# A hybrid decoder layer: other first loads, five-panel weight rings, and low-rank stages at other places of TensorE's order

## The chip, the cores and the metric

The kernel runs on one core of a Trainium2 chip. The metric is the time of one execution on the device in microseconds (us), and the smaller is the better. A core has a matrix engine (TensorE, called PE in the profile), a vector engine (VectorE, DVE), an engine for functions and copies (ScalarE, ACT), one for general work (GpSimd, POOL), and a synchronising engine (SyncE, SP) that here only issues transfers. They run side by side, each through its own list of instructions in order, and wait for each other by semaphores. Transfers from the device's memory (DMA) run beside all of them.

## The reference

One layer for 256 tokens of width 2048. A root-mean-square norm, one product into all branch inputs, four causal window averages (pooling), a recurrent mixer of 16 heads of 64 (RWKV-7), an output product, a squared-ReLU network of width 8192, and a gated embedding:

```
h = rms_norm(x, attn_norm);  z = h @ w_in
d = causal_multiscale_pool(z_pool);  pool_out = (d @ pool_w) * pool_scale
zs = token_shift(z[...], mu_shift)                # r, k, v and the low-rank w, a, g
y = rwkv7_time_mix(zs...)                         # state S <- S*w + (S a) b^T + v k^T,  y = S r
x = x + concatenate([pool_out, y]) @ w_out
x = x + square(relu(rms_norm(x, mlp_norm) @ w_ffn_up)) @ w_ffn_down
gate = sigmoid(rms_norm(x, ple_norm) @ w_ple_gate)
x = x + gate * (p @ w_ple_proj);  return rms_norm(x, final_norm)
```

All is computed in 32-bit floats.

## The kernel before

**Products.** A large product takes each 32-bit operand apart into a high part, rounded to TensorE's fast 32-bit type (fp32r), and the low rest, and adds three products: high by high, low by high, high by low. Weights come in panels of 512 KB, 128 partitions by 1024. `load_raw` issues the transfer on SP's queue, `split_w` (lines L157 to L166) makes the high part on ACT in two halves (`wh`, L165) and the low part on DVE (`wl`, L166). The buffers of raw, high and low panels are rings (`ring`): three of each, and one more of each once the mixer's memory is free, each fourth panel going there. A panel can be loaded when the last reader of the buffer's former panel is done.

**Stages.** The head (0 to 26.5 us of the trace) loads x transposed (`xT`, four panels of four k-tiles of 128 rows) and a narrow weight `wag` of 288 columns for the low-rank inputs w, a and g, multiplies them in plain 32-bit floats (`wag_prod`, two matmuls for each k-tile, which the trace shows as four records), squares x on DVE, sums the squares over partitions by four small matmuls (`sbank`), takes the root (`rs_n`), spreads the factors over partitions by two matmuls (`s_ps`, `s_bc`) and scales and splits x into `hTh` and `hTl`.

Then come the products of `w_in` in the order zk, zr for heads' group 0, zk, zr for group 1, zv0, zv1, zp0, zp1 (26.5 to 275). They are generators in a queue. Between their pieces the stages of the mixer are put: `fill(us)` issues products for about so many microseconds by the author's estimate, and `finish(gen)` all that is left of one. The stages of a group of eight heads are `rwkv_lora` (low-rank decay and a: two banks lw and la, sigmoids, a scan, two exponentials), `rwkv_k` (kkn, rnb), `rwkv_r`, `rwkv_scores` (sc), `rwkv_sources` (bkt), `bonus_sums` (bsum), `rwkv_values` (bon, vt), `rwkv_core` (us, dy), `group_norm`, and `group_out` (yt: a transposition). A triangular inverse runs on DVE beside them. A product's two banks are evacuated by `shift_evac` (L322 on ACT, L323 on DVE). Up to here TensorE's order is that of the code; DVE's and ACT's are set by a scheduler by priorities (`tc.high_priority`).

After the output product (287 to 384) the network goes in two halves. Each half has a product up (L1104, L1108; 384 to 564 and 731 to 911) and two sweeps down (`sweep`, 564 to 731 and 911 to 1068), over 16 pairs of panels. A plain pair (even ones, and 15) is split as above. A seven pair (odd ones from 1 to 13) uses seven products where eight would stand: `weights_seven` forms four combinations of its panels ra and rb on DVE (t1, which is two of them, L1226; t2, L1231; t3, L1232), and the parts `w7h`, `th` (ACT) and `w7l` (L1229, L1235), `tl` (L1236) (DVE). Behind the last seven pair, `u` combines the banks, and `scaled_residual` adds them to x, the wide one for 1024 columns at once. The gate's product and the end follow (1068 to 1191). Eight of the gate's panels are split early and kept (`keep`), in memory whose tags `keep_at` names.

Of the kernel before, what the change touches and what calls it, by code (L numbers as in the profile page):

```python
# [9 lines left out]
F32 = mybir.dt.float32  # L10
# [30 lines left out]
def trunk(  # L41
# [39 lines left out]
    def rw_bank(name):  # L81
        return psr.tile([128, 512], F32, tag="rw", name=name)
# [19 lines left out]
    nc.vector.memset(ones, 1.0)  # L102
# [227 lines left out]
    order.enter_context(tc.manual_schedule(engines={mybir.EngineType.PE}))  # L330
    wag_banks = [rw_bank(f"wag_b{i}") for i in range(2)]
# [20 lines left out]
    def load_wag(tag, k0, n, eng=nc.sync):  # L352
        wr = rp.tile([128, n, 288], F32, tag=tag, name=f"wag{k0}")
        eng.dma_start(wr, w_wag[:, k0 : k0 + n, :])
        return [wr[:, i, :] for i in range(n)]
# [8 lines left out]
    def load_wags(eng, *parts):  # L364
        for tg, k0, n in parts:
            wr.update(zip(range(k0, k0 + n), load_wag(tg, k0, n, eng)))
# [17 lines left out]
    for k in range(12):  # L384
        wag_prod(k)
# [6 lines left out]
    for k in range(12, 14):  # L392
        wag_prod(k)
# [14 lines left out]
    for k in range(14, NK):  # L408
        wag_prod(k)
# [602 lines left out]
    fill(14.0)  # L1012
    st0 = rwkv_lora(0)
    finish(p_zk0)
    wband = make_bands()
    rwkv_k(0, st0, zk0[0])
# [18 lines left out]
    finish(p_zv0)  # L1035
    fill(4.0)
    rwkv_values(0, st0, zv0[0])
    bonus_sums(1, st1)
# [15 lines left out]
    fill(4.0)  # L1054
# [98 lines left out]
    keep_at = ["ys"] * 3 + ["a5", "th", "tl", "t", "U"]  # L1153

    def keep():
# [3 lines left out]
        if where == "ys":  # L1159
            wh, wl = (fp.tile([128, 1024], F32R, tag=where, bufs=7, name=f"gk{kp}{c}") for c in "hl")  # L1160
# [55 lines left out]
    def weights_seven(ra, rb, name):  # L1216
# [7 lines left out]
        with tc.high_priority(20000):  # L1224
# [4 lines left out]
            nc.vector.tensor_tensor(la, ra, ha.bitcast(F32), op=ALU.subtract)  # L1229
# [269 lines left out]
```

## Time and profile before

| | us |
|---|---|
| three timed runs | 1195.39, 1196.88, 1192.28 |
| median | 1195.39 |
| the profiled execution's own time | 1192.48 |
| its span, first to last instruction | 1190.8 |
| busy in it: PE, DVE, ACT | 1164.7, 855.4, 678.7 |

The profile shows one execution. A line of the timeline gives start, time taken, engine, source line, operation, output and inputs with their shapes, how many instructions are grouped (x16), and in square brackets the idle time ahead of them and what ended it. A 32-bit matmul of the head is two records. A matmul's own time reaches into the next one's, so that the distance from start to start is its cost. PEclk is the share of TensorE's full clock that was granted.

### The profile page before, as it was taken

What the parts mean: (1) busy time and instruction counts of PE and PEld (TensorE: products, weight loads), DVE (VectorE), ACT (ScalarE), POOL (GpSimd) and SP (SyncE); (2) the same over time, 40 slices, a digit from 0 to 9 for tenths busy, and PEclk for the clock granted to TensorE, in tenths of its full rate; (3) what the DMA queues carried; (4) which work ended last, traced back from release to release, by engine and by line L of the source; (5) the groups of instructions that cost most, each with busy time, mean ns of one, the idle gap of its engine ahead of it and who ended that gap; (6) DMA issues with size and microseconds to landing.
All of it is one profiled execution on the core that took longest, in us unless ns stands there. A gap on an engine that the chain in (4) does not pass through costs nothing.

```text
span 1190.8 us, 18955 instructions
## 1 busy us (share of the span) xinstructions
PE 1164.7 (98%) x7366; PEld 996.4 (84%) x7366; DVE 855.4 (72%) x1073; ACT 678.7 (57%) x1210; POOL 20.1 (2%) x77
## 2 busy tenths in 40 slices
PE   7999999999999999999999999999999999999997
PEld 5899999787888888888878888888888788887886
DVE  6885799356655666667788887666668789888753
ACT  5956765667555554555554554554546554568643
POOL 4100000000000000000000000000000000000000
PEclk9999999999999999999999999999999999999999
DMA  7353434454566556565455656555555565666831
GB/s 267 124 187 124 155 125 142 143 175 138 191 184 191 178 180 191 182 190 182 172 212 185 217 204 210 193 181 190 185 187 163 208 208 186 218 246 201 274 125 71
DMA packets 60618, 216.92 MB, mean 182 GB/s; under 512 B 6768, under 2 KB 7536, under 8 KB 60144
## 3 DMA queue, kind: packets, MB, share of 16 engines
q1 hardware_dynamic: 60240, 215.20, 54.8%
q8 instruction: 58, 0.95, 0.3%
q10 hardware_dynamic: 288, 0.51, 0.1%
q14 instruction: 32, 0.26, 0.1%
HBM read 213.59 MB, written 2.10 MB: 181 GB/s over the span
## 4 chain that ended last, share of the span: by engine, by line
PE 73%; DVE 5%; DMA 2%; ACT 1%; issue 1%; DVEq 0%; ACTq 0%
PE u_w L1104 20%; PE d_p L1173 13%; PE u_w L1108 10%; PE d_w L1173 5%; PE d_d L1173 3%; PE o_b L188 2%; PE o_b L187 2%; PE o_b L189 2%; PE gt_b L187 2%; PE gt_b L189 2%; PE gt_b L188 2%; DVE wl_d L166 2%; DMA raw_d<-in_w_ffn_down_dram 2%; PE zp_b L187 1%; PE zp_b L189 1%
## 5 line engine op out<-in xcount | busy, mean ns | idle before, releaser
L1104 PE MATMUL u_w<-h,wh_u 128*128 128x512 f32 x1024 | 362.1, 399 | 0.0
L1108 PE MATMUL u_w<-h,wl_u 128*128 128x256 f32 x1024 | 287.7, 281 | 0.0
L165 ACT ACTIVATE wh_u<-raw_u 128x512 fp32r<-128x512 f32 x256 | 147.4, 624 | 175.6 <-issue 136.7
L166 DVE TENSOR_TENSOR wl_u<-raw_u,wh_u 128x1024 fp32r<-128x1024 f32 x128 | 156.6, 1224 | 120.9 <-ACT wh_u L165 120.9
L1104 PEld LDWEIGHTS u_w<-h,wh_u 128*128 128x128 f32 x1024 | 192.5, 188 | 47.8
L1108 PEld LDWEIGHTS u_w<-h,wl_u 128*128 128x128 f32 x1024 | 193.4, 189 | 0.0
L1173 PE MATMUL d_p<-wh_d,yd 128*128 128x512 f32 x432 | 115.6, 389 | 0.0
L1173 PEld LDWEIGHTS d_p<-wh_d,yd 128*128 128x128 f32 x432 | 81.0, 188 | 16.6
L165 ACT ACTIVATE wh_d<-raw_d 128x512 fp32r<-128x512 f32 x144 | 79.7, 619 | 23.4 <-PE d_d L1173 12.0
L166 DVE TENSOR_TENSOR wl_d<-raw_d,wh_d 128x1024 fp32r<-128x1024 f32 x72 | 85.1, 1219 | 2.3 <-ACT wh_d L165 2.2
L1236 DVE TENSOR_TENSOR tl_d<-t_d,th_d 128x2048 fp32r<-128x2048 f32 x28 | 64.2, 2292 | 29.3 <-ACT th_d L1234 29.3
L1173 PE MATMUL d_p<-wl_d,yd 128*128 128x512 f32 x216 | 68.5, 393 | 2.8 <-DVE wl_d L166 2.8
L1234 ACT ACTIVATE th_d<-t_d 128x1024 fp32r<-128x1024 f32 x28 | 29.7, 1060 | 69.1 <-DVE t_d L1232 69.1
L166 DVE TENSOR_TENSOR wl_o<-raw_o,wh_o 128x1024 fp32r<-128x1024 f32 x32 | 39.1, 1225 | 35.9 <-ACT wh_o L165 35.9
L165 ACT ACTIVATE wh_o<-raw_o 128x512 fp32r<-128x512 f32 x64 | 36.7, 624 | 32.4 <-PE o_b L188 18.4
L1173 PEld LDWEIGHTS d_p<-wl_d,yd 128*128 128x128 f32 x216 | 40.5, 188 | 14.2 <-DVE wl_d L166 6.1
L1226 DVE TENSOR_TENSOR t_d<-raw_d,raw_d 128x1024 f32<-128x1024 f32 x28 | 34.2, 1222 | 14.4 <-DMA raw_d<-in_w_ffn_down_dram 14.4
L1173 PE MATMUL d_w<-th_d,ys 128*128 128x512 f32 x168 | 42.6, 389 | 0.0
L1230 ACT ACTIVATE th_d<-t_d 128x1024 fp32r<-128x1024 f32 x28 | 29.7, 1060 | 17.9 <-DVE t_d L1226 14.7
L178 PE MATMUL zv_b<-hTh,wh_zv 128*128 128x256 f32 x128 | 37.8, 295 | 1.3 <-DVE zv_t L323 1.3
L178 PE MATMUL zr_b<-hTh,wh_zr 128*128 128x256 f32 x128 | 36.7, 287 | 2.0 <-DVE zk_t L323 2.0
L1173 PE MATMUL d_d<-wh_d,yd 128*128 128x512 f32 x144 | 38.5, 389 | 0.0
(445 smaller groups left out, 2529.5 us busy)
## 6 DMA issues: line engine op xcount, KB each, us to landing
raw_u<-in_w_ffn_up_dram SPq DMA_DIRECT2D x128, 512.0 KB, 3.5
raw_d<-in_w_ffn_down_dram SPq DMA_DIRECT2D x128, 512.0 KB, 4.4
raw_o<-in_w_out_dram SPq DMA_DIRECT2D x32, 512.0 KB, 3.5
raw_gt<-in_w_ple_gate_dram SPq DMA_DIRECT2D x24, 512.0 KB, 4.4
raw_zk<-in_w_in_dram SPq DMA_DIRECT2D x16, 512.0 KB, 4.1
raw_zr<-in_w_in_dram SPq DMA_DIRECT2D x16, 512.0 KB, 3.5
raw_zv<-in_w_in_dram SPq DMA_DIRECT2D x16, 512.0 KB, 3.5
raw_zp<-in_w_in_dram SPq DMA_DIRECT2D x16, 512.0 KB, 3.5
```

The source lines that it names most:

```text
L165: nc.scalar.activation(wh[:, a * 512 : (a + 1) * 512], raw[:, a * 512 : (a + 1) * 512], AF.Copy)
L166: nc.vector.tensor_tensor(wl, raw, wh.bitcast(F32), op=ALU.subtract)
L178: nc.tensor.matmul(o, w_h, ah, start=first and ct % 2 == 0, stop=False, skip_group_check=True)
L187: nc.tensor.matmul(o, a_h, wh[:, 0:n], start=first, stop=False)
L188: nc.tensor.matmul(o, a_l, wh[:, 0:n], start=False, stop=False)
L189: nc.tensor.matmul(o, a_h, wl[:, 0:n], start=False, stop=last)
L1104: nc.tensor.matmul(bank[:, ct, :].rearrange("p (s t) -> p s t", s=2), wh[:, c], hl, start=k == 0, stop=False, skip_group_check=True,)
L1108: nc.tensor.matmul(bank[:, ct, 0:T], wl[:, c], hl[:, 0, :], start=False, stop=k == 15, skip_group_check=True)
L1173: nc.tensor.matmul(o, l, r, start=first, stop=last, skip_group_check=True)
L1226: nc.vector.tensor_tensor(t[:, 0:2], ra.rearrange("p (c n) -> p c n", c=2), b12.unsqueeze(1).to_broadcast([128, 2, 512]), op=ALU.subtract)
L1230: nc.scalar.activation(th[:, 0:2], t[:, 0:2], AF.Copy)
L1236: nc.vector.tensor_tensor(tl, t, th.bitcast(F32), op=ALU.subtract)
```

## The change

It has three parts.

1. *Head.* `ones` is written earlier; nine matmuls of `ones` by `ones` into a bank of their own stand ahead of TensorE's other work. The first x^T panel comes in two halves, the first three k-tiles of wag as two (on ACT's queue) and one; the last two x^T panels are issued ahead of wag's k-tiles 9 to 11. The four matmuls of the norm's sum stand behind eleven k-tiles of wag, not twelve, the two of s_ps behind thirteen, not fourteen.
2. *Rings and the sweeps.* Raw, high and low panels have three buffers and two more (low: one more) after the mixer. `u` uses the memory of t, and `keep_at` another place in the list. In `weights_seven` the DVE part of ra's low half stands behind t2 and t3. The wide residual's priority is 25000, not 10000.
3. *Mixer's order.* `rwkv_lora(0)` stands behind the end of zk0, `rwkv_lora(1)` ahead of `rwkv_sources(0)`, `bonus_sums(1)` right behind the end of zv0; three fill times differ.

```diff
-    nc.vector.memset(ones, 1.0)
+    with tc.high_priority(40000):
+        nc.vector.memset(ones, 1.0)
...
+    RING = {"raw": (3, 2), "wh": (3, 2), "wl": (3, 1)}
     def ring(tag, dt, name):
-        if extra:
-            turns[tag] += 1
-            if turns[tag] % 4 == 0:
-                return extra[0].tile([128, 1024], dt, tag=f"{tag}x", name=name)
-        return wp.tile([128, 1024], dt, tag=tag, name=name)
+        n, m = RING[tag]
+        turns[tag] += 1
+        if extra and turns[tag] % (n + m) >= n:
+            return extra[0].tile([128, 1024], dt, tag=f"{tag}x", bufs=m, name=name)
+        return wp.tile([128, 1024], dt, tag=tag, bufs=n, name=name)
...
+    warm_bank = rw_bank("warm_b")
+    for i in range(9):
+        nc.tensor.matmul(warm_bank[:, 0:128], ones, ones, start=True, stop=True)
...
+    def load_wag(tag, k0, n, eng=nc.sync, first=0):
+        wr_ = rp.tile([128, n, 288], F32, tag=tag, name=f"wag{k0}")
+        if first:
+            nc.scalar.dma_start(wr_[:, 0:first], w_wag[:, k0 : k0 + first, :])
+        eng.dma_start(wr_[:, first:n], w_wag[:, k0 + first : k0 + n, :])
+        return [wr_[:, i, :] for i in range(n)]
...
-    load_wags(nc.scalar, ("tE", 0, 3))
-    load_xT(0, 0, 4)
-    load_wags(nc.sync, ("tF", 3, 3))
+    load_xT(0, 0, 2)
+    load_wags(("tE", 0, 3), first=2)
+    load_xT(0, 2, 2)
+    load_wags(("tF", 3, 3))
     load_xT(1, 0, 4)
-    load_wags(nc.sync, ("zk", 6, 3))
+    load_wags(("zk", 6, 3))
     load_xT(2, 0, 4)
-    load_wags(nc.sync, ("zr", 9, 3))
     load_xT(3, 0, 4)
-    load_wags(nc.sync, ("zv", 12, 2), ("BK", 14, 2))
+    load_wags(("zr", 9, 3), ("zv", 12, 2), ("BK", 14, 2))
...
-    for k in range(12):
+    for k in range(11):
         wag_prod(k)
...
-    for k in range(12, 14):
+    for k in range(11, 13):
...
-    for k in range(14, NK):
+    for k in range(13, NK):
...
-    fill(14.0)
-    st0 = rwkv_lora(0)
     finish(p_zk0)
     wband = make_bands()
+    fill(3.0)
+    st0 = rwkv_lora(0)
+    fill(3.0)
     rwkv_k(0, st0, zk0[0])
...
     rwkv_scores(0, st0)
+    st1 = rwkv_lora(1)
     rwkv_sources(0, st0)
     bonus_sums(0, st0)
-    st1 = rwkv_lora(1)
     finish(p_zk1)
     rwkv_k(1, st1, zk1[0])
-    fill(12.0)
+    fill(13.0)
     rwkv_scores_half(1, st1, 0)
...
     finish(p_zv0)
+    bonus_sums(1, st1)
     fill(4.0)
     rwkv_values(0, st0, zv0[0])
-    bonus_sums(1, st1)
...
-    fill(4.0)
+    fill(5.3)
     for gi in range(2):
         group_out(gi, 1, norms[1][gi], YTs[gi])
...
-    keep_at = ["ys"] * 3 + ["a5", "th", "tl", "t", "U"]
+    keep_at = ["ys"] * 3 + ["yd", "a5", "th", "tl", "t"]
...
-            nc.vector.tensor_tensor(la, ra, ha.bitcast(F32), op=ALU.subtract)
-            nc.scalar.activation(th[:, 0:2], t[:, 0:2], AF.Copy)
             nc.vector.tensor_tensor(t[:, 2], b22, t[:, 0], op=ALU.add)
             nc.vector.tensor_tensor(t[:, 3], b21, t[:, 2], op=ALU.subtract)
+            nc.scalar.activation(th[:, 0:2], t[:, 0:2], AF.Copy)
             nc.scalar.activation(hb[:, 0:512], b21, AF.Copy)
+            nc.vector.tensor_tensor(la, ra, ha.bitcast(F32), op=ALU.subtract)
+            nc.vector.tensor_tensor(lb[:, 0:512], b21, hb[:, 0:512].bitcast(F32), op=ALU.subtract)
             nc.scalar.activation(th[:, 2:4], t[:, 2:4], AF.Copy)
-            nc.vector.tensor_tensor(lb[:, 0:512], b21, hb[:, 0:512].bitcast(F32), op=ALU.subtract)
...
-                    u = fp.tile([128, 4, 512], F32, tag="U", name=f"u_{name}")
+                    u = fp.tile([128, 4, 512], F32, tag="t", name=f"u_{name}")
...
-        with tc.high_priority(10000 if wide > 512 else 30000):
+        with tc.high_priority(25000 if wide > 512 else 30000):
```

Line numbers of the changed kernel are higher by 2 to 9: the splits L165 and L166 are L167 and L168, t1, t2, t3 are L1235, L1238, L1239, the low halves L1242 and L1243.

The first place is ACT's list in the head, from the last scaling of x^T (tD) to the first high part of h; `wh_zk_0`, `_1` and `_2` are the first three panels of zk. Before:

```order
L341 ACTIVATE tD_t<-xq_204,par_sb 128x256 x4
L165 ACTIVATE wh_zk_0_343<-raw_zk_0_341 128x512 x2
L165 ACTIVATE wh_zk_1_374<-raw_zk_1_372 128x512 x2
L165 ACTIVATE wh_zk_2_426<-raw_zk_2_424 128x512
L398 ACTIVATE rs_n_288<-sbank,eps_n 128x2
L165 ACTIVATE wh_zk_2_426<-raw_zk_2_424 128x512
L407 ACTIVATE s_bc<-s_ps 128x256
L170 ACTIVATE hTh_152<-tA_t 128x256 x2
```

And in the changed kernel:

```order
L346 ACTIVATE tD_t<-xq_214,par_sb 128x256 x4
L405 ACTIVATE rs_n_298<-sbank,eps_n 128x2
L167 ACTIVATE wh_zk_0_355<-raw_zk_0_353 128x512 x2
L167 ACTIVATE wh_zk_1_386<-raw_zk_1_384 128x512
L414 ACTIVATE s_bc<-s_ps 128x256
L167 ACTIVATE wh_zk_1_386<-raw_zk_1_384 128x512
L172 ACTIVATE hTh_152<-tA_t 128x256
L167 ACTIVATE wh_zk_2_438<-raw_zk_2_436 128x512
L172 ACTIVATE hTh_152<-tA_t 128x256
L167 ACTIVATE wh_zk_2_438<-raw_zk_2_436 128x512
```

The norm's root (`rs_n`) has moved ahead of all of zk's high parts, which so start behind sbank, and the first two k-tiles of h are taken one by one between the parts of the third panel.

The second place is TensorE's list ahead of the second half of the groups' outputs (`yt`), from the last window average (`pd`) to the gates (`gt`); `zp_b` is the last product of the queue. Before:

```order
L951 MATMUL pd_3391<-wband,zt_2918 128x128
L890 MATMUL yt<-ident,ys_2746 128x128 x4
L890 MATMUL yt<-ident,ys_2747 128x128 x4
L187 MATMUL zp_b_2928<-wh_zp_7_3330,hTh_153 128x512
L188 MATMUL zp_b_2928<-wh_zp_7_3330,hTl_155 128x512
L189 MATMUL zp_b_2928<-wl_zp_7_3331,hTh_153 128x512
L187 MATMUL zp_b_2928<-wh_zp_7_3330,hTh_153 128x512
L188 MATMUL zp_b_2928<-wh_zp_7_3330,hTl_155 128x512
L189 MATMUL zp_b_2928<-wl_zp_7_3331,hTh_153 128x512
L890 MATMUL yt<-ident,ys_2746 128x128 x4
L890 MATMUL yt<-ident,ys_2747 128x128 x4
L909 MATMUL gt<-zf,gu_2715 128x256 x4
```

And in the changed kernel:

```order
L958 MATMUL pd_3411<-wband,zt_2911 128x128
L897 MATMUL yt<-ident,ys_2764 128x128 x4
L897 MATMUL yt<-ident,ys_2765 128x128 x4
L897 MATMUL yt<-ident,ys_2764 128x128 x4
L897 MATMUL yt<-ident,ys_2765 128x128 x4
L916 MATMUL gt<-zf,gu_2733 128x256 x4
```

The six products of zp between the two halves of yt are gone from here; they stand ahead of the places shown, and no product of the queue is left for `fill(5.3)`.

The third place is DVE's list in the first sweep down, around the plain pair 8 and the seven pair 9: `t_d_9` are t1, t2 and t3, `wl_d_0_8` and `wl_d_1_8` the low parts of pair 8, `w7l_d_9` and `tl_d_9` those of pair 9. Before:

```order
L1236 TENSOR_TENSOR tl_d_7_6248<-t_d_7_6246,th_d_7_6247 128x2048
L166 TENSOR_TENSOR wl_d_0_8_6289<-raw_d_0_8_6284,wh_d_0_8_6288 128x1024
L166 TENSOR_TENSOR wl_d_1_8_6294<-raw_d_1_8_6286,wh_d_1_8_6293 128x1024
L1226 TENSOR_TENSOR t_d_9_6326<-raw_d_0_9_6322,raw_d_1_9_6324 128x1024
L1229 TENSOR_TENSOR w7l_d_9_6331<-raw_d_0_9_6322,w7h_d_9_6329 128x1024
L1231 TENSOR_TENSOR t_d_9_6326<-raw_d_0_9_6322,t_d_9_6326 128x512
L1235 TENSOR_TENSOR w7l_d_9_6332<-raw_d_1_9_6324,w7h_d_9_6330 128x512
L1232 TENSOR_TENSOR t_d_9_6326<-raw_d_1_9_6324,t_d_9_6326 128x512
L1236 TENSOR_TENSOR tl_d_9_6328<-t_d_9_6326,th_d_9_6327 128x2048
```

And in the changed kernel:

```order
L1245 TENSOR_TENSOR tl_d_7_6260<-t_d_7_6258,th_d_7_6259 128x2048
L1235 TENSOR_TENSOR t_d_9_6338<-raw_d_0_9_6334,raw_d_1_9_6336 128x1024
L1238 TENSOR_TENSOR t_d_9_6338<-raw_d_0_9_6334,t_d_9_6338 128x512
L168 TENSOR_TENSOR wl_d_0_8_6301<-raw_d_0_8_6296,wh_d_0_8_6300 128x1024
L168 TENSOR_TENSOR wl_d_1_8_6306<-raw_d_1_8_6298,wh_d_1_8_6305 128x1024
L1239 TENSOR_TENSOR t_d_9_6338<-raw_d_1_9_6336,t_d_9_6338 128x512
L1242 TENSOR_TENSOR w7l_d_9_6343<-raw_d_0_9_6334,w7h_d_9_6341 128x1024
L1243 TENSOR_TENSOR w7l_d_9_6344<-raw_d_1_9_6336,w7h_d_9_6342 128x512
L1245 TENSOR_TENSOR tl_d_9_6340<-t_d_9_6338,th_d_9_6339 128x2048
```

t1 and t2 of pair 9 have moved ahead of pair 8's low parts, and the low part of pair 9's first panel behind t3. In the first sweep of each half this is so at the seven pairs 3, 5, 7, 9, 11 and 13 (t1 and t2 ahead of both low parts, or of the first), in the second at 11 and 13; before, t1 alone was ahead at 3, 5, 7 and 11, and in the second sweep at 11.

More of the change, by code (lines that the diff above doesn't have):

```diff
@@ L350, in squares @@
         return sq
[L352 to L355, printed above, removed]
+    def load_wag(tag, k0, n, eng=nc.sync, first=0):
[4 more added lines that the diff above has]
+        return [wr_[:, i, :] for i in range(n)]
     def wag_prod(k):
@@ L362, in wag_prod, with load_wags @@
             )
[L364 removed]
+    def load_wags(*parts, first=0):
         for tg, k0, n in parts:
[L366 removed]
+            wr.update(zip(range(k0, k0 + n), load_wag(tg, k0, n, nc.sync, first)))
     wr = {}
[L369 to L371 removed]
+    load_xT(0, 0, 2)
+    load_wags(("tE", 0, 3), first=2)
+    load_xT(0, 2, 2)
+    load_wags(("tF", 3, 3))
     load_xT(1, 0, 4)
[L373 removed]
+    load_wags(("zk", 6, 3))
     load_xT(2, 0, 4)
[L375 removed]
     load_xT(3, 0, 4)
[L377 removed]
+    load_wags(("zr", 9, 3), ("zv", 12, 2), ("BK", 14, 2))
     sums = []
@@ L1158, in keep @@
         raw = load_raw(w_gate[3, kp].rearrange("p a n -> p (a n)"), 1024, f"gk{kp}")
-        if where == "ys":
-            wh, wl = (fp.tile([128, 1024], F32R, tag=where, bufs=7, name=f"gk{kp}{c}") for c in "hl")
+        if where[0] == "y":
+            wh = fp.tile([128, 1024], F32R, tag="ys", bufs=7, name=f"gk{kp}h")
+            wl = fp.tile([128, 1024], F32R, tag=where, bufs=7 if where == "ys" else 1, name=f"gk{kp}l")
         else:
```

## The prediction

> **What bounds the kernel now.** I read the page first (share of each engine), then the waits of TensorE, then the stages by windows, then single places in the timeline. Columns of the waits: who waits at which line, for whom, us in total, times, longest.
>
> ```profile
> span 1190.8 us, 18955 instructions
> PE 1164.7 (98%) x7366; PEld 996.4 (84%) x7366; DVE 855.4 (72%) x1073; ACT 678.7 (57%) x1210; POOL 20.1 (2%) x77
> PE wag_b L359 <- DMA wag<-in_w_wag_dram: 7.8, 1, 7.8
> PE d_p L1173 <- DVE wl_d L166: 2.8, 6, 0.6
> PE zr_b L178 <- DVE zk_t L323: 2.0, 1, 2.0
> PE sc L642 <- DVE AR L584: 1.4, 1, 1.4
> PE zv_b L178 <- DVE zv_t L323: 1.3, 1, 1.3
> PE yt L890 <- DVE gv L883: 1.2, 1, 1.2
> ```
>
> TensorE (PE) is busy 98% of the span, so 1190.8 - 1164.7 = 26.1 us is all that its waits can give back, and 7.8 of them are the start. The change adds or removes no product of the body: its gain must come out of these 26 us, out of products that ran at half clock, or both.
>
> ```profile
> core 0: us, PE busy (x) PEld busy (x) DVE busy (x) ACT busy (x) POOL busy (x), PEclk, DMA share, GB/s
> 112.00:206.00 94.00, 91.28 (x963) 87.42 (x963) 81.52 (x144) 58.96 (x109) 1.12 (x2) 0.98 0.41 135
> 384.00:564.00 180.00, 180.00 (x1023) 156.25 (x1022) 120.06 (x162) 96.66 (x179) 0.00 (x0) 1.00 0.59 185
> 564.00:648.00 84.00, 82.94 (x364) 67.84 (x363) 69.44 (x66) 45.42 (x67) 0.00 (x0) 1.00 0.55 188
> ```
>
> In the FFN-up stage (384 to 564) PE has no gap at all: deeper rings and other orders can change nothing there. The waits lie in the head, in the mixer (27 to 287) and in the four FFN-down sweeps, the first from 564 to 648. I go through these.
>
> **The head, part 1 of the change.** Timeline of PE: start, time taken, what.
>
> ```profile
> 7.84 6.09 PE L359 MATMUL wag_b<-wag,tA_t 128*128 128x288 f32 x16 [7.84 <-DMA wag<-in_w_wag_dram]
> 13.77 4.04 PE L359 MATMUL wag_b<-wag,tB_t 128*128 128x288 f32 x16
> 17.65 4.04 PE L359 MATMUL wag_b<-wag,tC_t 128*128 128x288 f32 x16
> 21.53 0.95 PE L388 MATMUL sbank<-ones,sqx 128*128 128x1 f32 x8
> 24.36 0.61 PE L406 MATMUL s_ps<-dgs,ones 128*128 128x128 f32 x4
> 26.54 0.49 PE L178 MATMUL zk_b<-hTh,wh_zk 128*128 128x256 f32 x1
> ```
>
> The second row's sixteen records start 17.65 - 13.77 = 3.88 us before the third, 0.2425 each; the first row's take 13.77 - 7.84 = 5.93. So 2.05 us go to a half-speed clock at the start. From 7.84 on PE never waits until zk. In the changed kernel 64 records of 0.2425 (15.5), sbank's 0.8 and s_ps's 0.45 are the same work, 16.8 us; only the start and the cold clock move. The first pieces are two k-tiles of x^T (256 KB in place of 512) and two of wag (288 KB in place of 432), on two queues as before; I put the first product at 6.7, between 7.84, where a smaller load brings nothing, and 6.0, where the row of ACT below has its first scaled k-tile (start 5.60, a quarter of 1.70), with parameters and x^T there but for the weights; 6.7 because the weights, the last to land, are a third smaller. The nine products of ones are 18 records; at twice s_ps's 0.11 they run from the end of the memset, 1.2, to about 5.2. If they leave the clock at full speed, zk starts at 6.7 + 16.8 = 23.5. ACT and DVE must follow:
>
> ```profile
> 5.60 1.70 ACT L341 ACTIVATE tA_t<-xq,par_sb 128x256 f32<-128x256 f32 x4 [2.86 <-DMA par_sb<-in_par_dram]
> 16.70 0.42 DVE L383 TENSOR_TENSOR sqx<-sqx,sqx 128x256 f32<-128x256 f32 x1
> 25.01 0.38 ACT L407 ACTIVATE s_bc<-s_ps 128x256 f32<-128x256 f32 x1 [1.71 <-PE s_ps L406]
> ```
>
> The squares end at 17.1 and sbank now comes after eleven k-tiles, 6.7 + 44 x 0.2425 = 17.4: no wait. In the new order rs_n stands ahead of zk's weight splits on ACT, and one split of DVE (1.2 us) ahead of the low half of h: s_ps 20.7, s_bc 21.2, product 21.8, split 23.0, low half 23.7. So zk is fully fed at about 23.6: **-2.9 us**, bounds -0.9 (clock still cold) and -3.6 (first product at 6.0).
>
> [...]
>
> **The mixer, part 3.** Four waits are touched.
>
> ```profile
> 49.99 1.28 ACT L530 ACT_TABLE_LOAD   x1
> 51.36 1.06 ACT L530 ACTIVATE tA_t<-tB_t 128x1024 f32<-128x1024 f32 x1
> 118.11 1.28 ACT L530 ACT_TABLE_LOAD   x1
> 126.48 1.28 ACT L543 ACT_TABLE_LOAD   x1
> 54.32 0.28 PE L180 MATMUL zr_b<-hTh,wl_zr 128*128 128x256 f32 x1
> 56.59 0.39 PE L178 MATMUL zr_b<-hTh,wh_zr 128*128 128x256 f32 x1 [1.99 <-DVE zk_t L323]
> 137.52 0.28 PE L180 MATMUL zv_b<-hTh,wl_zv 128*128 128x256 f32 x1
> 139.19 2.00 PE L642 MATMUL sc<-AR,BK 64*128 64x64 f32 x32 [1.39 <-DVE AR L584]
> 142.88 0.41 PE L178 MATMUL zv_b<-hTh,wh_zv 128*128 128x256 f32 x1
> 274.67 0.40 PE L189 MATMUL zp_b<-wl_zp,hTh 128*128 128x512 f32 x1
> 276.28 0.63 PE L890 MATMUL yt<-ident,ys 128*128 128x128 f32 x4 [1.22 <-DVE gv L883]
> ```
>
> (1) zr's second bank (56.59) waits for the evacuation of zk's first, which sits on ACT behind lora's sigmoids, a table load and two exponentials. In the new order lora(0) stands 27 products behind zk's last, so the evacuations come first: **-2.1** (0 if lora's work runs into the next evacuation instead).
>
> (2) sc (139.19) waits for AR, at the end of a chain through k(1), while ACT loads its table four times, for lora(1) and k(1) in turn (first and last are the rows 118.11 and 126.48). lora(1) now stands ahead of sources(0), so its exponentials are over when k(1) begins, which takes two of the four loads (2 x 1.28) and lora's own work off that chain; fill(13) adds one us of cover. 1.4 of waiting against 2.6 + 1.0: the wait goes, with its tail **-1.5**. Behind it PE ran at half clock: products of 0.41 in place of 0.28 (row 142.88), and the window's clock of 0.98. (1 - 0.98) x 94 gives 1.9; sixteen products some 0.09 late give 1.5. I hold the idle time to be its cause: **-1.5**, bounds 0 and -1.9.
>
> [...]
>
> (3) The second bank of zv's second part waits 1.3 for DVE, which evacuates the first part behind the inverse's steps. bonus_sums(1), four products of up to 256 columns that stood behind it, now stands ahead of it, as cover: 0.5 by products of 0.12 us, and the rest if DVE's steps shift with it. I take **-0.7**, bounds 0 and -1.3.
>
> (4) yt waits for the group norm. Before, six zp products (1.4 us) stood between its two halves. The new order has none left there, as it used them up earlier; fill(5.3) finds an empty queue. The norm's chain is as long as before, so the wait grows by those six: **+1.4**. A pause of some 2.7 us can re-gate the clock as at 139: half a chance of 1.6, **+0.8**.
>
> (5) lora(0) inside zr leaves fewer products between rnb and scores(0): 99 where 159 stood. No row shows that wait; the nearest is the same wait of group 1, 1.4, below it nothing: **+0.4**.
>
> **FFN down, part 2.** DVE, the loop of one seven pair (odd) and a plain pair (even), 593 to 599, and ACT's next start; ahead of them the two loads' rows of the page, their last column the us from issue to landing:
>
> ```profile
> raw_u<-in_w_ffn_up_dram SPq DMA_DIRECT2D x128, 512.0 KB, 3.5
> raw_d<-in_w_ffn_down_dram SPq DMA_DIRECT2D x128, 512.0 KB, 4.4
> 587.37 0.69 DVE L1232 TENSOR_TENSOR t_d<-raw_d,t_d 128x512 f32<-128x512 f32 x1
> 593.19 1.23 DVE L1226 TENSOR_TENSOR t_d<-raw_d,raw_d 128x1024 f32<-128x1024 f32 x1 [1.72 <-DMA raw_d<-in_w_ffn_down_dram]
> 594.33 2.35 DVE L166 TENSOR_TENSOR wl_d<-raw_d,wh_d 128x1024 fp32r<-128x1024 f32 x2
> 598.94 0.68 DVE L1232 TENSOR_TENSOR t_d<-raw_d,t_d 128x512 f32<-128x512 f32 x1
> 604.92 0.63 ACT L1233 ACTIVATE w7h_d<-raw_d 128x512 fp32r<-128x512 f32 x1 [1.86 <-DMA raw_d<-in_w_ffn_down_dram]
> ```
>
> The stall reads so: DVE's t1 (L1226) waits for its panel, the plain pair's low halves (L166) stand behind it, and PE waits for those. A panel is issued when the last reader of its buffer is done: with four buffers t3 (L1232) of the seven pair before, 588.1, landed 593.2: 5.1 us; the next 599.6 to 604.9, 5.3. From t1 to t3's end are 6.4 us, so a pair of pairs with t1 first takes 11.4 or more, against PE's 45 products (24 in a plain pair, 21 in a seven pair) of 0.228 (82.94 us by 364, the windows' row) = 10.3; where L166 comes first it takes less, and on average DVE keeps up. Six stalls of 0.5 to 0.6 (the waits' row), with restarts some 4.6 us in all.
>
> The new order puts t1 and t2 ahead of both low halves at 16 of the 28 seven pairs, where t1 alone was ahead at ten. With five buffers the panel that t1 needs waits for the high pair's low half (L1229), which stands behind t1, t2, two L166 and t3: all that fills the 6.4 us now but one half panel (0.6), so 5.8 to 5.9. The two panels of a pair are no longer issued together. With the median landing, 4.4, the loop is 10.3, PE's own, with nothing to spare: I allow 0.16 at each of 16 places, 2.6; with 3.5, the landing in the stage without waits, it is 9.4 and no stall is left. From 4.6 to 2.6: **-2.0**, bounds -4.6 and, at 5.3 (0.9 over in 16 places, 14.4), +9.8.
>
> The scale's higher priority for wide residuals and u in t's place put DVE's work at a sweep's end a few us earlier or later beside products of the other banks; I see no wait there now and take 0, as for keep's new places, which PE reads 80 us later.
>
> **Sum.** -2.9 - 2.1 - 1.5 - 1.5 - 0.7 + 1.4 + 0.8 + 0.4 - 2.0 = -8.1. The profiled execution took 1192.48 (span 1190.8 and 1.7 around it), which gives 1184.4. It lies 2.9 below the median of the three timed runs, 1195.39; a median of new runs may sit anywhere in that spread, so I add half of it: **1185.8**.
>
> **Rivals.** (a) The clock stays or falls cold: the products of ones end about 1.5 us before the first wag product. Then the head gives 0.9: 1187.8. For it: the half clock behind 139.19 after as short a pause. Against: that pause had sparse products ahead.
> (b) The mixer makes new waits: scores(0) at the full 1.4 in place of 0.4, zv's kept (0.7), yt's clock lost in full (0.8), together 2.5 more: 1188.3. For it: lora's table load is only moved, beside another chain.
> (c) The rings do not do what they are for: DVE's order is static, t1 stays ahead, stalls remain 4.6: 1187.8.
> (d) **Slower than before**: DVE's t1 and t2 at the head of the line. A landing of 5.3, as twice above, makes the loop 11.2, 0.9 over PE's at 16 places: +9.8 where I have -2.0, so 1197.6, and more where it is longer still. It decides from a landing of about 5.1, where 0.7 at 16 places less the 4.6 are +6.6 and eat up the rest of the gain. For it: 5.1 and 5.3 are what this loop shows now. Against it: both were panels issued right behind their partners, which five buffers take apart.
>
> **How the numbers follow.** A measurement of this kernel can tell about 0.5%, 6 us, from no change; faster means below 1189.4, slower above 1201.4. Forecast 0.45, (a) 0.17, (b) 0.15, (c) 0.13, (d) 0.10. (b) lies close to the line, a third of it beyond; (d) lies inside it but for landings above 5.5. Faster 0.78, same 0.18, slower 0.04. The range takes the favourable bounds (head 0.7, FFN 2.6, yt's clock 0.8, zv 0.6 better and the fast half of the spread, 1.5: about 1179.6) and above it (a) to (c) two at a time, and a part of (d): 1192.5.
>
> **What would show it.** Right: zk's first product near 23.6; the second sixteen records no slower than the first; no wait at zr's second bank or at sc; one wait of 2.5 to 3 at yt; d_p's wait for wl_d below 2. Wrong: wag's first row at 5.9 again (a); a wait at the scores of group 0 (b); six or more waits of d_p (c), or some sixteen with t_d waiting for raw_d by over 1 us each (d).

## The result, and the profile after

| | before | changed |
|---|---|---|
| median of 12 runs each, us | 1195.13 | 1189.31 |
| lowest to highest | 1191.08 to 1196.88 | 1187.06 to 1192.90 |
| ratio, 95% interval | | 0.9961 [0.9948, 0.9974] |
| profiled execution's own time | 1192.48 | 1192.90 |

The change is faster by 0.39%, 4.7 us (the ratio is that of the means; the medians lie 5.8 apart), within the 6 us that the prediction called no change; the forecast had 8 to 10. The two profiled executions happen to take the same time, since that of before is one of its faster ones and that of the changed kernel its slowest. So the profiles show where time moved, and the timed runs how much it is.

The waits of TensorE in the changed kernel (who waits at which line, for whom, us in total, times, longest):

```profile
PE yt L897 <- DVE gv L890: 3.3, 1, 3.3
PE zk_b L180 <- DVE zr_t L325: 2.2, 1, 2.2
PE zr_b L180 <- DVE zk_t L325: 1.9, 1, 1.9
PE zp_b L189 <- DVE zv_t L325: 1.6, 1, 1.6
PE warm_b L335 <- DVE ones L103: 1.2, 1, 1.2
PE rnb L496 <- DVE rnq L560: 0.9, 2, 0.7
PE us L852 <- ACT UV L845: 0.9, 1, 0.9
PE vt L776 <- DVE ybuf L762: 0.9, 1, 0.9
PE zv_b L180 <- DVE zv_t L325: 0.4, 1, 0.4
PE wag_b L366 <- DMA wag<-in_w_wag_dram: 0.3, 1, 0.3
PE d_p L1182 <- DVE wl_d L168: 0.2, 1, 0.2
```

The start's 7.8 and the sweeps' 2.8 are gone, and sc's 1.4. zr's 2.0, which was to go, is still there. New are waits at zk's second bank, zp, rnb and us; vt's has grown from 0.2 to 0.9 and yt's from 1.2 to 3.3. All of them lie in the mixer. The stages of the same profile:

```profile
27.00:112.00 85.00, 80.74 (x718) 76.62 (x716) 61.31 (x93) 58.87 (x114) 3.78 (x12) 0.96 0.43 142
112.00:206.00 94.00, 90.54 (x917) 86.02 (x915) 81.50 (x142) 55.62 (x107) 1.12 (x2) 1.00 0.44 142
206.00:287.00 81.00, 76.86 (x1127) 62.23 (x1127) 38.78 (x51) 52.34 (x113) 0.00 (x0) 0.98 0.47 161
564.00:648.00 84.00, 84.00 (x378) 69.67 (x377) 70.38 (x67) 46.86 (x68) 0.00 (x0) 1.00 0.59 200
```

The window of the first sweep has no idle time left (84.00 of 84.00, where 82.94 stood). Behind three pauses of the mixer (at zr, zk and yt) PE ran a stretch of 3.4 us at half clock each (granted 0.50 from 51.3, 82.0 and 280.0 on), so its granted clock (the eighth column) is 0.96 and 0.98 where before had 1.00, 0.98, 1.00 in these three stretches. The head:

```profile
1.15 4.21 PE L335 MATMUL warm_b<-ones 128*128 128x128 f32 x18 [1.15 <-DVE ones L103]
5.66 4.72 PE L366 MATMUL wag_b<-wag,tA_t 128*128 128x288 f32 x16 [0.30 <-DMA wag<-in_w_wag_dram]
10.21 4.04 PE L366 MATMUL wag_b<-wag,tB_t 128*128 128x288 f32 x16
17.00 0.95 PE L395 MATMUL sbank<-ones,sqx 128*128 128x1 f32 x8
22.98 0.50 PE L180 MATMUL zk_b<-hTh,wh_zk 128*128 128x256 f32 x1
```

wag starts at 5.66, and its first sixteen records take 10.21 - 5.66 = 4.55 us, the next sixteen 3.88 (before: 5.93 and 3.88); zk starts 26.54 - 22.98 = 3.56 us earlier. But the output product starts at 291.39 where it started at 286.43: the mixer takes 8.5 us longer in this execution than in that of before.

### The profile page after: what moved, and what is told of

The parts are those of the page before. It is cut to its first block, busy times and chain, and to the rows that moved or that the text cites. A ratio compares the mean times of both kernels' runs of the same rounds, so it can differ in the third digit from the quotient of the medians.

```text
span 1191.2 us, 18959 instructions
## 1 busy us (share of the span) xinstructions
PE 1169.1 (98%) x7384; PEld 1002.4 (84%) x7384; DVE 857.2 (72%) x1073; ACT 674.8 (57%) x1208; POOL 17.1 (1%) x77
## 4 chain that ended last, share of the span: by engine, by line
PE 85%; DVE 6%; ACT 4%; DMA 2%; issue 1%; POOL 0%; DVEq 0%; ACTq 0%; POOLq 0%
PE u_w L1112 20%; PE d_p L1182 15%; PE u_w L1116 10%; PE d_w L1182 6%; PE d_d L1182 4%; PE o_b L190 2%; PE o_b L189 2%; PE o_b L191 2%; PE gt_b L191 2%; PE gt_b L190 2%; PE gt_b L189 2%; PE wag_b L366 1%; DMA raw_d<-in_w_ffn_down_dram 1%; PE zp_b L189 1%; PE zp_b L191 1%
## 5 line engine op out<-in xcount | busy, mean ns | idle before, releaser
L167 ACT ACTIVATE wh_u<-raw_u 128x512 fp32r<-128x512 f32 x256 | 147.2, 624 | 161.6 <-issue 138.4
L168 DVE TENSOR_TENSOR wl_u<-raw_u,wh_u 128x1024 fp32r<-128x1024 f32 x128 | 156.4, 1224 | 104.9 <-PE u_w L1116 84.5
L167 ACT ACTIVATE wh_d<-raw_d 128x512 fp32r<-128x512 f32 x144 | 82.4, 622 | 66.4 <-PE d_d L1182 40.4
L168 DVE TENSOR_TENSOR wl_d<-raw_d,wh_d 128x1024 fp32r<-128x1024 f32 x72 | 85.5, 1220 | 5.8 <-ACT wh_d L167 3.0
L1182 PE MATMUL d_p<-wl_d,yd 128*128 128x512 f32 x216 | 66.9, 390 | 0.2 <-DVE wl_d L168 0.2
L168 DVE TENSOR_TENSOR wl_o<-raw_o,wh_o 128x1024 fp32r<-128x1024 f32 x32 | 39.2, 1224 | 33.3 <-PE o_b L191 20.3
L167 ACT ACTIVATE wh_o<-raw_o 128x512 fp32r<-128x512 f32 x64 | 36.8, 624 | 33.5 <-issue 15.3
L1235 DVE TENSOR_TENSOR t_d<-raw_d,raw_d 128x1024 f32<-128x1024 f32 x28 | 34.2, 1222 | 16.7 <-DMA raw_d<-in_w_ffn_down_dram 16.7
L1234 ACT ACTIVATE w7h_d<-raw_d 128x1024 fp32r<-128x1024 f32 x28 | 29.5, 1053 | 25.8 <-PE d_d L1182 24.3
L180 PE MATMUL zk_b<-hTh,wh_zk 128*128 128x256 f32 x128 | 38.0, 297 | 2.2 <-DVE zr_t L325 2.2
L168 DVE TENSOR_TENSOR wl_zp<-raw_zp,wh_zp 128x1024 fp32r<-128x1024 f32 x16 | 19.6, 1223 | 27.6 <-ACT wh_zp L167 26.4
```

The lines of the kernel that those rows point to most:

```text
L167: nc.scalar.activation(wh[:, a * 512 : (a + 1) * 512], raw[:, a * 512 : (a + 1) * 512], AF.Copy)
L168: nc.vector.tensor_tensor(wl, raw, wh.bitcast(F32), op=ALU.subtract)
L180: nc.tensor.matmul(o, w_h, ah, start=first and ct % 2 == 0, stop=False, skip_group_check=True)
L1182: nc.tensor.matmul(o, l, r, start=first, stop=last, skip_group_check=True)
L1235: nc.vector.tensor_tensor(t[:, 0:2], ra.rearrange("p (c n) -> p c n", c=2), b12.unsqueeze(1).to_broadcast([128, 2, 512]), op=ALU.subtract)
```

## The experiments

Fifteen kernels, in four groups; each ratio is against runs of before on the same chip at the same time. First the three parts apart. `mixer_old` is the changed kernel with the mixer's order of before (all lines of the diff's third part undone):

> The changed kernel with the mixer's order of before (part 3 undone; head, rings and sweeps as changed). Theory A: the head's 3.5 us and the sweeps' 4.5 us of the trace are real and last, and the new order of the mixer gives about 3.3 of them back; then this kernel is 8 us faster than before, ratio about 0.9933. Theory B: the mixer's order is neutral and the head's or the sweeps' gain is lost on its way (an earlier start runs into a later load, the clock); then this kernel is like the changed one, ratio about 0.996. zr's wait of 2 us and sc's of 1.5 are back in both.

0.9933 [0.9914, 0.9953]: theory A to the digit. The head and the rings are worth 8 us, and the mixer's new order costs about 3 of them (the two intervals just meet).

`rings_only`, `head_only` and `mixer_only` have one part of the diff each.

> Before with the rings, u in t's memory and the sweeps' new order alone. Theory A: the waits of d_p for wl_d (2.8 us, 4.6 with restarts) go as in the changed kernel, -4.5 us, ratio 0.9962. Rival: the sweeps' waits went because the sweeps started at another phase against their loads, and return here in part: -2 or less.

> Before with the new head alone. Theory A: zk starts at about 23.0 instead of 26.5 and everything follows, -3.5 us, ratio 0.9971. Rival: the products' weights, which come no faster, or the clock give part of it back before the mixer: -1.5 or less, with the wait visible on zk or at lora.

> Before with the mixer's new order alone. Theory A: +3 to +4 us, ratio 1.0025 to 1.0035: waits of 2 us each at zr's, zk's second banks and at zp, 3.3 at yt, against sc's 1.5 that is gone. Theory B: within 1 us of before. The forecast on record had -3 (without head and sweeps).

Measured: rings 0.9931 [0.9904, 0.9958], head 0.9991 [0.9978, 1.0005], mixer 1.0016 [1.0003, 1.0030]. The rings give more than the trace had shown, the head nearly nothing, and the mixer's order alone is slower, by less than expected: of the waits named, zr's isn't in the list of `mixer_only` at all. With the new order it takes the new head to make that wait, 1.9 in the changed kernel. The row of waits of `head_only` tells more:

```profile
PE zr_b L179 <- DVE zk_t L324: 4.3, 1, 4.3
PE d_p L1179 <- DVE wl_d L167: 2.9, 6, 0.6
```

That is `head_only`: zk starts at 22.94, but zr's second bank, which waited 2.0 before, now waits 4.3, and the products behind it start 0.21 us apart (55.68 to 57.81) where those ahead of it start 0.12 apart; in before the granted clock is 1.00 behind the same wait (54.3 to 60.0). The mean granted clock is 0.994 in this profile and 0.997 in that of before. PE came earlier; the evacuation that it waits for didn't. What holds it beside lora is GpSimd's and DVE's making of the pool's bands. The timelines of GpSimd in before and then in `head_only`:

```profile
41.08 0.38 POOL L128 MEMSET wband<- 128x144 f32 x2 [18.95 <-ACT zf L449]
```

```profile
41.25 0.38 POOL L129 MEMSET wband<- 128x144 f32 x2 [20.59 <-DVE tD_t L423]
```

The bands lie in the memory of `s_bc` (one tag, "wband"), so they begin when the last k-tiles of h have been scaled (`tD_t`, whose scaling ends at 40.9 in before and 41.1 in head_only; the ACT row that the first line names is another). That is 41 us with either head, and the DVE list has them, zr's low parts and lora's scans ahead of zk's evacuation. The second group tests that, and takes the rings apart.

`after_bands` and `old_bands` (from the changed kernel and from mixer_old) make the bands late, tied to zv1's result:

```
-    def make_bands():
+    def make_bands(gate):
         wband = mc.tile([128, 4, 272], F32, tag="wband", name="wband")
+        nc.gpsimd.tensor_copy(wband[:, :, ::144], gate[:, :, 0:2])
...
-    wband = make_bands()
...
     rwkv_values(1, st1, zv1[0])
+    wband = make_bands(zv1[0])
```

> The changed kernel, the pool's bands (wband) built later: their first write on GpSimd copies two columns of zv1's result, so that it waits for it, and the twelve small DVE instructions leave the place ahead of zk's evacuation. Theory A: the evacuation of zk's first bank, due at about 45.6, then follows at once: zr's wait of 2.1 falls below 0.6, with it the half-clock window behind it; 2 to 3 us off the changed kernel, ratio to before 0.9935 to 0.9945. The wait at zk's second bank (2.3, on zr's evacuation behind k(0)'s chain on DVE) and yt's 3.3 stay. Rival: the wait only moves to the next evacuation, 0.996 as the changed kernel.

> The head, rings and sweeps of the change, the mixer's order of before, and the bands built later. Theory A: the 3.5 us that the head wins end at zr's second bank, whose wait grew from 2.0 to 4.3 since the bands' place in DVE's list is tied to a time (41 us) and not to TensorE: without them the wait falls to 2.0 or less, and one of two half-clock windows goes: 2.3 to 4 us off mixer_old, ratio to before 0.990 to 0.9915. Rival: lora's scans and table load alone hold the evacuation: no change against mixer_old, 0.993.

after_bands: 0.9935 [0.9916, 0.9954]. zr's wait isn't in its list any more, and the profile's mean granted clock is 0.995 where the changed kernel's is 0.994; zk's 2.2 and yt's 3.2 are in the list, as expected. In time the two intervals of it and of the changed kernel overlap, and its median is only 0.4 us lower, so the size is open. old_bands: 0.9924 [0.9904, 0.9943], with zr's wait at 2.3 in place of 4.3: the bands were the two us that the earlier head had added, and lora's scans and table load are the other 2. The time is between the two theories.

`rings_depth` has the rings, u and keep_at alone, `sweep_order` the order in weights_seven and the residual's priority alone:

> Before with five-panel rings, u in t's memory and keep's new places, but weights_seven's order and the residual's priority of before. Theory A: the waits came from panels issued too late, a matter of the rings' depth alone: most of the gain of rings_only (0.9931) is here, 0.994 or lower, and d_p waits under 1 us. Rival: the order in weights_seven does it: 0.998 to 1.

> Before with the new order in weights_seven and the wide residual's priority alone, four-panel rings. Theory A: no gain, since the panel of the next seven pair still comes late: 0.998 to 1.002, d_p waits six times or more. Rival: the earlier t2 and t3 free the panel earlier, and the order alone brings -3 us or more, 0.9975 or lower.

0.9935 [0.9915, 0.9955] and 1.0000 [0.9985, 1.0015]; d_p waits 0.3 us in the first, 3.2 in nine waits in the second. It is the depth; the order brings nothing.

The third group goes into the mixer. `fill12`, from after_bands:

```
-    fill(13.0)
+    fill(12.0)
     rwkv_scores_half(1, st1, 0)
```

> after_bands with fill(12) ahead of the first scores of group 1, as before, in place of fill(13). Theory A: the one us of products that fill(13) takes ahead of the inverse is missing behind it, where nothing else covers the chain to yt: from the merge (gm) to the output product (o_b) after_bands takes 91.0 us where before takes 86.4; six zp products come back between the two halves of yt, whose wait falls from 3.2 to 1.2 to 1.9, and zp's 1.6 and us's 1.5 shrink: 88.5 or less, 2 to 3 us off after_bands, ratio to before about 0.9915; sc does not wait, as lora(1) is done. Rival: sc waits again (1.0 or more) and takes it back: 0.9935 as after_bands.

0.9890 [0.9869, 0.9912]: 4.5 thousandths, 5 us off after_bands, from one number, and more than the 2 to 3 expected. yt waits 1.4, zp and us no longer, sc doesn't wait.

`lora0_back`, from after_bands:

```
-    finish(p_zk0)
-    fill(3.0)
-    st0 = rwkv_lora(0)
-    fill(3.0)
+    fill(14.0)
+    st0 = rwkv_lora(0)
+    finish(p_zk0)
```

> after_bands with lora(0) ahead of zk's end as before (fill 14). Theory A: with lora(0) late, k(0)'s DVE chain falls onto zr's evacuation, which is zk's wait of 2.2 (and rnb's 0.4) with the half-clock window behind it; both go, and the wait at zr's second bank is back at 2: 0 to 2 us off after_bands, ratio 0.992 to 0.9935. Rival: zk's wait of 2.2 stays, which then has another cause, and the time is 2 us worse than after_bands.

0.9950 [0.9931, 0.9970]. The waits changed places as theory A has it (zk's second bank no longer in the list, zr's at 2.3), but the time is not lower: lora(0)'s late place is worth nothing or a little.

`lora1_only`, from old_bands, moves `st1 = rwkv_lora(1)` ahead of `rwkv_sources(0, st0)` and nothing else:

> old_bands with lora(1) ahead of sources(0) alone, fill(12) kept. Theory A: two table loads leave k(1)'s chain, sc's wait of 1.4 goes (to under 0.4) with its half-clock window, and the inverse starts and ends 1.5 us earlier: 1.5 to 3 us off old_bands, ratio 0.990 to 0.991. Rival: the wait moves to another place behind it, no change, 0.9925.

0.9906 [0.9886, 0.9926], sc's wait of 1.4 gone; the mean granted clock is 0.997 in this profile and in that of old_bands. From zk's start to the merge it takes 172.9 us in the trace against 173.8 of old_bands, and 2 us less in time, with intervals that overlap widely: the move is probably good by itself, but its size isn't shown.

`no_warm` is old_bands without the nine products of ones:

> old_bands without the nine products of ones. Theory A: wag's first eight records run at half clock again, 1.9 us later at zk (about 24.9); but zr's wait of 2.3, set by DVE's and ACT's lora chain, takes most of it back, so within 1 us of old_bands, ratio 0.992 to 0.9935. Rival: the whole 2 us show: 0.994.

0.9915 [0.9894, 0.9936], no slower than old_bands. The profile of old_bands is one in which they did not help: from wag's first product to sbank it took 12.9 us, like no_warm's 13.0, and 10.7 to 11.4 in the nine other profiles that have them. So the two us are there at zk nine times in ten, and in the version where lora holds zr's bank they don't show at the end.

The last group settles what was open: `after_fill12` is the changed kernel with that one number changed, `fill12_no_head` is fill12 with the head of before, `fill12_k_early` is fill12 without the fill(3.0) behind `rwkv_lora(0)`.

> The changed kernel with nothing undone but fill(13) ahead of group 1's first scores, which is fill(12) again. Theory A: this one number cost some 4 to 5 us of the change (products missing as cover behind the inverse, gm to o_b 90.6 us where 86.4 is possible, and the half clock behind the long wait at yt): 4 us or more off the changed kernel, ratio to before 0.9925 or lower. Rival: the gain of fill12 came from its other bands, or from chance in the up product's pace: 0.995 or above.

> fill12 with the head of before (no products of ones, the first loads of before). Theory A: where no fixed wait stands behind the head any more, its 3.5 us are real: 3 to 4 us slower than fill12, ratio to before 0.9915 to 0.993. Rival: the head's gain is lost again at another evacuation: within 1 us of fill12, 0.989 to 0.990.

> fill12 without the fill(3) behind lora(0), so that k(0) starts 3 us of products earlier. Theory A: k(0)'s DVE chain is then over before zr's last panel, the wait at zk's second bank (2.2) falls to under 0.6: 1.5 to 2.5 us off fill12 (1181.6), ratio to before 0.987 to 0.9875. Rival: the evacuation is as late for ACT's and DVE's other work: no change, 0.989.

after_fill12: 0.9910 [0.9896, 0.9924], against the changed kernel's 0.9961: fill(13) alone cost 5 us by the medians, 6 by the ratios. From the merge (`gm`) to the output product (`o_b`), in windows of before, of the changed kernel and of after_fill12 (length, PE busy, and so on):

```profile
200.07:286.43 86.36, 84.73 (x1242) 68.22 (x1242) 46.34 (x62) 57.37 (x122) 0.00 (x0) 1.00 0.49 158
```

```profile
200.75:291.39 90.64, 84.91 (x1234) 68.53 (x1234) 47.41 (x65) 57.38 (x121) 0.00 (x0) 0.98 0.44 148
```

```profile
197.13:283.61 86.48, 84.78 (x1243) 68.22 (x1242) 46.32 (x63) 57.23 (x122) 0.00 (x0) 1.00 0.50 157
```

PE's busy time is the same, 84.7 to 84.9; the changed kernel has 5.7 us of pauses in it, the others 1.7. It also has nine products of zv (1.1 us) less in this window, those that fill(13) takes ahead of it, and loses about as much to the half clock behind yt. The place at yt in the timeline of the changed kernel and then of after_fill12:

```profile
275.68 1.04 PE L897 MATMUL yt<-ident,ys 128*128 128x128 f32 x8
280.00 1.94 PE L897 MATMUL yt<-ident,ys 128*128 128x128 f32 x8 [3.28 <-DVE gv L890]
281.73 2.49 PE L916 MATMUL gt<-zf,gu 128*128 128x256 f32 x7
```

```profile
269.81 1.04 PE L897 MATMUL yt<-ident,ys 128*128 128x128 f32 x8
270.60 0.48 PE L189 MATMUL zp_b<-wh_zp,hTh 128*128 128x512 f32 x1
...
273.46 0.63 PE L897 MATMUL yt<-ident,ys 128*128 128x128 f32 x4 [1.22 <-DVE gv L890]
274.30 0.63 PE L897 MATMUL yt<-ident,ys 128*128 128x128 f32 x4 [0.21 <-DVE ys L891]
274.76 1.89 PE L916 MATMUL gt<-zf,gu 128*128 128x256 f32 x8
```

The second half of yt costs 1.94 us where the first costs 1.04: half clock (granted 0.50 from 280.0 to 283.4) behind a pause of 3.3. In after_fill12 zp's products stand between the halves again. The two profiles are 10 us apart in all: 4.2 us in this window, and 3.4 each from two things that stand ahead of fill(13) or far behind it, the half-clock stretches at zr and zk (the mean granted clock is 0.994 in the changed kernel's profile and 0.998 in that of after_fill12) and the pace of the product up (last section). So the window, and not the whole profile, measures fill(13).

fill12_no_head: 0.9915 [0.9899, 0.9930] against fill12's 0.9890: the head is worth 2.5 thousandths, 3 us, where nothing behind it takes them (medians 1184.91 and 1181.55; the ranges and the intervals overlap in part). The profiles agree: without the head zk starts 4.5 us later (27.42 for 22.89) and the output product 4.7 us later (285.94 for 281.24). fill12_k_early: 0.9886 [0.9871, 0.9902], no different from fill12, and the wait at zk's second bank is still 2.0. Its DVE timeline:

```profile
72.80 1.22 DVE L169 TENSOR_TENSOR wl_zk<-raw_zk,wh_zk 128x1024 fp32r<-128x1024 f32 x1
73.93 1.22 DVE L587 TENSOR_TENSOR BK<-tF_t,tC_t 128x1024 f32<-128x1024 f32 x1
75.07 1.22 DVE L169 TENSOR_TENSOR wl_zk<-raw_zk,wh_zk 128x1024 fp32r<-128x1024 f32 x1
76.20 0.48 DVE L326 SCALAR_TENSOR_TENSOR zr_t<-zr_b,par_sb,zr_t 128x255 f32<-128x255 f32 x1
76.60 1.20 DVE L589 SCALAR_TENSOR_TENSOR AR<-tB_t,tA_t 128x1008 f32<-128x1008 f32 x1
77.71 0.87 DVE L326 SCALAR_TENSOR_TENSOR zr_t<-zr_b,par_sb,zr_t 128x255 f32<-128x255 f32 x2
```

ACT had its half of the first evacuation done at 73.9. DVE, busy without a gap, has four instructions of its list between that time and the last of the pieces (L326) that free the bank: two of k(0) (BK and AR) and two low parts of zk's weights. So the theory holds in part only: k(0)'s work is half of what stands ahead, and three us of lead are not enough, since the list's order moves along with them. lora0_back, with rnb 5 us earlier than after_bands, was free of it.

The fastest measured are fill12 and fill12_k_early, 1181.55 and 1180.90 us, 1.1% below before; they have all three parts of the change, but fill(12) and late bands.

## Why the prediction was wrong, point by point

The step that failed is the sum of the mixer's terms: forecast at -3.2 us (-2.1 - 1.5 - 1.5 - 0.7 + 1.4 + 0.8 + 0.4), measured at +2 alone (mixer_only) and +3 with the other two parts (mixer_old). Within it the largest mis-sized term is that of the missing products at yt, +2.2, which cost 5 (after_fill12). The rings erred the other way, -2.0 forecast and about -8 measured. That the two errors cancel in part, and the total came as near as it did, is luck.

**The head** (-2.9). In the trace right, and a little more: zk at 22.98, not 23.6, as wag could start at 5.66, ahead of my bound of 6.0. What failed is the step that took the gain at zk for a gain at the end. I had taken zr's wait for lora's alone and thought it gone by lora's move, and did not ask what else stood there that an earlier start doesn't move: the bands, at 41 us. Alone the head gave 0.1%, not clear of nothing, and 3 us only in fill12.

**zr's second bank** (-2.1). Wrong: 2.0 became 1.9. With the old head the term came true (mixer_only has no such wait). With the new one lora did leave its place, and the bands took it: DVE's list has all twelve of their pieces, waiting for GpSimd, and two low parts ahead of the evacuation (L325, the last row), whose first ACT half was done at 46.1:

```profile
45.51 0.28 DVE L132 TENSOR_TENSOR wband<-wband,ident 128x128 f32<-128x128 f32 x1
45.71 1.21 DVE L168 TENSOR_TENSOR wl_zr<-raw_zr,wh_zr 128x1024 fp32r<-128x1024 f32 x1
46.84 0.48 DVE L134 TENSOR_TENSOR wband<-wband,ident 128x128 f32<-128x128 f32 x2
47.25 0.16 DVE L133 TENSOR_TENSOR wband<-wband,edge 128x16 f32<-128x16 f32 x1
47.45 0.29 DVE L134 TENSOR_TENSOR wband<-wband,ident 128x128 f32<-128x128 f32 x1
47.66 1.22 DVE L168 TENSOR_TENSOR wl_zr<-raw_zr,wh_zr 128x1024 fp32r<-128x1024 f32 x1
48.79 0.48 DVE L325 SCALAR_TENSOR_TENSOR zk_t<-zk_b,par_sb,zk_t 128x255 f32<-128x255 f32 x1
```

after_bands shows the wait gone. The prediction asked only whether the evacuation stood ahead of lora.

**sc and the half clock behind it** (-1.5, -1.5). The wait went, shown also by lora1_only. The clock's loss only moved: three half-clock stretches stand behind the pauses at zr, zk and yt. Pauses of 1.9, 2.2 and 3.3 us were each followed by 3.4 us at a granted clock of 0.50, as sc's 1.4 was in before. But not every such pause was: behind zr's 2.0 in before the clock stayed at 1.00, and after_fill12, with the same 1.9 and 2.2 at zr and zk, has a mean granted clock of 0.998. A stretch costs 1.7 us and stands behind some pauses only (last section); my 0.8 for a chance of one was too small for three.

**zv** (-0.7). Right: 1.3 to 0.4.

**yt** (+1.4, and 0.8 for the clock). This is the mis-sized term. I saw that six zp products were missing there, and priced that place alone. They were missing because fill(13) spends one us of products ahead of the inverse, and behind the inverse everything is a chain of ACT and DVE that those products cover: zp waits 1.6, us 0.9, yt 2.1 more, and a half-clock stretch follows (280.0 to 283.4). Together, less the one us of products that left it, 4.3 us in the window above, 5 in time (after_fill12), for the 2.2 that I had. That I called fill(13) "one us of cover" for sc was half of the sentence: the us is taken from elsewhere, and sc no longer needed it.

**scores(0)** (+0.4). No wait there; the chain of k(0) came to bear on zr's evacuation in its place, which made zk's second bank wait 2.2, with a half-clock stretch (82.0 to 85.4). No rival named that place.

**FFN down** (-2.0). The direction was right, the size a quarter: -7.8 and -8.2 us by the ratios of rings_depth and rings_only. In the trace the favourable bound came, -4.6: all stalls went. The step that failed is the loop. I compared its length with PE's pace, 10.3, and thought that five panels shorten it to that. In the first sweep of a half, where four of the six stalls of before lay, it is hardly shorter: its six loops take 67.6 us in before (t1 from 558.7 to 626.3) and 66.9 in the changed kernel (560.2 to 627.1), 11.2 each, one us more than PE takes. (In the second sweep the loops are shorter, 9.6 us for 10.9.) t1 still waits for its panel, up to 2.6 us:

```profile
593.87 1.23 DVE L1235 TENSOR_TENSOR t_d<-raw_d,raw_d 128x1024 f32<-128x1024 f32 x1 [0.69 <-DMA raw_d<-in_w_ffn_down_dram]
605.72 1.23 DVE L1235 TENSOR_TENSOR t_d<-raw_d,raw_d 128x1024 f32<-128x1024 f32 x1 [2.34 <-DMA raw_d<-in_w_ffn_down_dram]
```

What the deeper rings change there is the lead with which DVE enters the sweep: its first t1 is 8.9 us ahead of PE's first product where it was 5.2. Before, and then the changed kernel:

```profile
558.70 1.23 DVE L1226 TENSOR_TENSOR t_d<-raw_d,raw_d 128x1024 f32<-128x1024 f32 x1 [0.16 <-DMA raw_d<-in_w_ffn_down_dram]
563.88 0.40 PE L1173 MATMUL d_p<-wh_d,yd 128*128 128x512 f32 x1
```

```profile
560.20 1.22 DVE L1235 TENSOR_TENSOR t_d<-raw_d,raw_d 128x1024 f32<-128x1024 f32 x1
569.10 0.40 PE L1182 MATMUL d_p<-wh_d,yd 128*128 128x512 f32 x1
```

Six loops lose some 5 to 6 us of it, which 8.9 can bear and 5.2 can't. All profiles agree: the lead is 5.0 to 5.2 in the four without the rings, with six to nine waits of d_p each, and 8.0 to 8.9 in the thirteen with them, with none to two. So rival (d)'s slow loop was there, at 11.2 as priced, and cost nothing. In the traces the four sweeps together are 5.0 us shorter (means of the four profiles and of the thirteen); the rest of the 8 is below.

**The rivals.** (a), a slow start of wag: once in ten profiles (old_bands, 12.9 us from its first product to sbank). (b), new waits in the mixer: it is what happened, but apart from yt's clock at other places (zk, zp, us) than it names, and with 5 us in place of 2.5. (c) and (d) fell.

The sum by the runs, each part alone: rings -8.2, head -1.1, mixer's order +1.9; they add up to -7.4 for the -4.7 measured. The intervals allow for that difference, and zr's wait, which the head and the order make only together, is in it.

## What to carry to other kernels

A filler product moved ahead of a long chain is taken from behind it: before moving one, look at the waits behind the chain that it covers now. When a stage starts earlier, look for the instruction behind it that is tied to something else, such as memory shared with another tile, since the gain can end there. For a queue of loads that is slower than its reader for a few rounds, count the lead that the buffers give at the start, not the round's length alone.

## What the runs showed of the hardware that was not expected

**The product up** runs a whole half at one of two paces without a wait in either. The same window of the stage, in before and in rings_depth:

```profile
L1104 PE MATMUL u_w<-h,wh_u 128*128 128x512 f32 x397 | 140.3, 399 | 0.0
```

```profile
L1105 PE MATMUL u_w<-h,wh_u 128*128 128x512 f32 x405 | 140.4, 391 | 0.0
```

In the 140 us from 400 to 540 one gets through 405 of the wide products and the other through 397. From one wide product's start to the next one's, with a narrow one between, it takes 140 us / 397 = 353 ns in before and 140 / 405 = 346 there; the first half's 512 pairs make some 3.5 us. Of the thirteen profiles with the five-panel rings six had the faster pace in the first half (rings_depth, old_bands, no_warm, fill12, after_fill12, fill12_k_early; the first two with 405 in this window, where the changed kernel has 397), of the four without them none; the second half has the slower pace in before and in the changed kernel (398 wide products in the 140 us from 750 to 890). What decides it was not tried. It would account for part of why the rings gave more in the timed runs than the sweeps' 5.0 us; that is argued, not shown. Two profiles can differ by 3 us from this alone (fill12 has the faster pace, after_bands and fill12_no_head the slower; from the output product's start to the end fill12's profile takes 896.0 us and that of fill12_no_head 899.0), and presumably so can two executions, so that ratios of five or six of them carry some of it.

**The clock** was granted at half behind some pauses and stayed full behind others. In the changed kernel it was 0.50 for 3.4 us from 51.3, 82.0 and 280.0 on, behind pauses of 1.9, 2.2 and 3.3 us that ended at 50.35, 81.82 and 280.00; in before from 141.5 to 145.0, behind sc's 1.4, which ended at 139.19. The products there start 0.21 us apart in place of 0.12, so a stretch of 3.4 us costs 1.7. In before zr's pause of 2.0, which ended at 56.59, cost nothing (1.00 from 54.3 to 60.0), nor did zp's 1.6 in the changed kernel (1.00 from 85.5 to 279.9). In fill12_k_early the products behind the pause of 2.0 at zk, which ended at 78.25, start 0.12 apart until 79.30 and 0.20 to 0.22 apart from 79.42 on. So the length of a pause alone did not tell what it cost: 1.4 us lost clock in before, and 2.0 did not. What decides it was not tried.
